# The last output product of a hybrid SSD/attention layer: who multiplies by the final norm weight, where the first two row tiles are finished, and which queue stores them

## The chip, the core and the metric

The kernel runs on one core of one Trainium2 chip. The time is device microseconds of one execution; the kernel before was run three times, and the median of these is what a change is measured against. Profiles come from one further execution each. The kernel uses five engines side by side, each with its own list of instructions in the order in which they were compiled: PE (TensorE, matrix products; the profile lists its weight loads as PEld), DVE (VectorE, elementwise), ACT (ScalarE, functions and scaled copies), POOL (GpSimd, elementwise) and SP (SyncE, which here only starts transfers). In this kernel ACT, POOL and SP start transfers (DMA). On-chip tiles have 128 partitions; PE's results go to eight banks of 128x512 float32.

## The reference

One layer with two branches (a state-space branch and an attention branch), both in float32, merged with gates, then one output product, a residual and a final RMSNorm. What matters here is only the end:

```python
merged = jax.nn.sigmoid(g_ssm) * (y @ w_proj_ssm) + jax.nn.sigmoid(g_attn) * (o @ w_proj_attn)
x = x + merged @ w_out                                  # (512, 2048) @ (2048, 2048)
y = x * lax.rsqrt(jnp.mean(x * x, axis=-1, keepdims=True) + EPS)
out = y * final_norm_w                                  # (512, 2048)
```

Each row of the output thus needs the sum of squares over all its 2048 columns before any part of it can be finished: the row factor r is one number for each row, the final weight one number for each column.

## The kernel before

**Tiles.** The 512 rows are four row tiles t = 0..3 of 128 rows, the 2048 columns four blocks b = 0..3 of 512. `res[t, b]` is one such 128x512 tile of x + merged @ w_out, kept on chip until the end. `ssf[:, t, b]` holds its sums of squares.

**Precision.** Each float32 operand is split into a rounded part h (a cast on ACT, line 433, written `wh`) and the rest l (a subtraction on DVE, line 434, written `wl`); a product is three matmuls (h·h, h·l, l·h). A weight chunk is 128x1024; PE can't use it before ACT has made `wh` and DVE has made `wl`. Each of these has three buffers.

**The output product.** Blocks 0 and 1 are made plainly (lines 1608-1624). Blocks 2 and 3 are made by Strassen's method with seven products instead of eight, in the order P1, P5, P6, P2, P3, P7, P4 (`Strassen.pair(1)`, lines 664-732), each of 48 matmuls on two banks with four weight chunks. P2 completes tiles (0,2) and (1,2), P3 completes (0,3) and (1,3), P7 completes (2,3) and (3,3), P4 completes (2,2) and (3,2). Each completed tile goes through `done_o` (lines 1642-1646): add x (line 1644), sum of squares on ACT (line 1576), `weigh`. The tiles of x for t < 2 are fetched by POOL into a three-buffer ring shared with the scratch of the squares (`fetch_o`, line 1632; the profile writes `gate<-x`); for t >= 2 they come with the final weight into one tile `fw` (`final_weights`, lines 1648-1655), which ACT's queue loads after P2.

P3 and P7 share the chunks Y: P3 uses each one, then POOL starts a transfer that adds a further block of w_out into it in place (line 505, `Y<-wo`), and P7 splits the sum again. P4 is made row tile by row tile (`product_rows`): its weights are split well ahead into `keep`, the first bank (t = 2) is complete half-way, the second (t = 3) at the end.

**The finish.** `weigh(t, b)` multiplies res[t, b] by the final weight on POOL (line 1571), in place, for all tiles but (2,2) and (3,2); the tiles of blocks 0 and 1 wait in the list `unweighed` until the weight is there and are all issued after P2. `finish(t)` sums the four sums of squares, makes r with a square root on ACT and a few one-column operations on DVE (lines 1659-1663, 185-191), scales the four tiles by r (two on DVE, two on ACT) and starts four stores of 256 KB, two from SP and two from ACT (line 1672). Row tiles 0 and 1 are finished in `before` of `last_o`, ahead of P4's sums and in an order that may not be changed (`pinned`); row tiles 2 and 3 as their banks of P4 complete (`each`).

**Order.** PE's order is written out by hand. All other engines' orders are made by a planner ahead of time: it walks through the program with a cost model, and whenever an engine is free in that model it takes, of the instructions that the model has ready, the one earliest in the program. `tc.high_priority(offset=n)` lets an instruction count as standing n instructions earlier (60 for the splits, `AHEAD`); `tc.keep_in_program_order` pins one. On the chip each engine then keeps this order, whatever really becomes ready first.

Of the kernel before, what the change touches and what calls it, by code (L numbers as in the profile page):

```python
# [15 lines left out]
ALU = mybir.AluOpType  # L16
AX = mybir.AxisListType

P = 128
D = 2048  # L20
SEQ = 512
# [51 lines left out]
def build(tc, a):  # L73
    nc = tc.nc
    act, dve, pool, pe = nc.scalar, nc.vector, nc.gpsimd, nc.tensor
# [25 lines left out]
    def few(n):  # L101

        n_small[0] += n
        assert n_small[0] <= 96
        return small[:, n_small[0] - n:n_small[0]]
# [36 lines left out]
    def mm(n="mm"):  # L142
        return ps.tile([P, SEQ], F32, tag="mm", bufs=3, name=n)

    def pa(n="pa"):
        return ps.tile([P, SEQ], F32, tag="pa", bufs=2, name=n)

    def pb(n="pb"):
        return ps.tile([P, SEQ], F32, tag="pb", bufs=2, name=n)

    def pc(n="pc"):
        return ps.tile([P, SEQ], F32, tag="pc", bufs=1, name=n)
# [50 lines left out]
    for t in range(TT):  # L203
# [7 lines left out]
        v = few(1)  # L211
# [169 lines left out]
    def st(name):  # L381
        return gp.tile([P, SEQ], F32, tag="st", bufs=3, name=name)
# [147 lines left out]
    def sum_tile(tag):  # L530

        if tag == "kk" or tag == "u" and kk:
            return kk.tile([P, SEQ], F32, tag="kk", bufs=2, name=tag)
        return part_.tile([P, SEQ], F32, tag=tag, bufs=2, name=tag)
# [14 lines left out]
    def product_done():  # L549
        for e in later:  # L550
            e[0] -= 1
        while later and later[0][0] <= 0:
            later.popleft()[1]()
# [31 lines left out]
    def product_rows(name, op, chunk, keep, each, pre):  # L585

        used.append((used[-1] + 1) % 4)
        bs = [b(name) for b in SETS[used[-1]]]
        for m in range(4):
            with tc.high_priority(offset=AHEAD):  # L590
                split_into(keep[0][:, m], keep[1][:, m], chunk(m))
        pre()
        for i in range(2):
            for j in range(8):
                xh, xl = op(0, j, i), op(1, j, i)
                wh, wl = (t[:, j // 2, j % 2 * 512:(j % 2 + 1) * 512] for t in keep)
                pe.matmul(bs[i], xh, wh, start=(j == 0), stop=False)
                pe.matmul(bs[i], xh, wl, start=False, stop=False)
                pe.matmul(bs[i], xl, wh, start=False, stop=(j == 7))
                yield 3  # L600
            each(i, bs[i])
# [275 lines left out]
    def rsqrt1(v):  # L877

        return small_rsqrt(v, 1, lambda n: hi.tile([P, 1], F32, tag={"rt": "mx", "rr": "nm"}[n], bufs=4, name=n))
# [490 lines left out]
    def place(shape, name):  # L1370

        n = n_places[0] % 5
        n_places[0] += 1
        return xb.tile(shape, F32R, tag="opb" if n else "opc", bufs=4 if n else 1, name=name)
# [58 lines left out]
    m_ops, m_op = Ops(m_d), {}  # L1433
# [112 lines left out]


    ssf = few(16).rearrange("p (t b) -> p t b", t=TT)
    res, room, unweighed = {}, {}, []

    def x_of(t, b):
        return a["x"][t * P:(t + 1) * P, b * SEQ:(b + 1) * SEQ]

    def out_chunk(acc, t, kc, h, l, start, stop):

        for k in range(2):
            kk_ = kc * 2 + k
            op = m_ops.view[f"x{t // 2 + 1}{kk_ // 8 + 1}"]
            mh, ml = (op(s_, kk_ % 8, t % 2) for s_ in range(2))
            wh, wl = (w_[:, k * SEQ:(k + 1) * SEQ] for w_ in (h, l))  # L1560
            pe.matmul(acc, mh, wh, start=(start and k == 0), stop=False)
            pe.matmul(acc, mh, wl, start=False, stop=False)
            pe.matmul(acc, ml, wh, start=False, stop=(stop and k == 1))

    def w_out(cg, kc):
        return w_split(w_load(w_tile("w"), "wo", 0, kc // 4, cg, kc % 4))

    def weigh(t, b):
        if t < 2 or b != 2:
            if "fw" in room:  # L1570
                pool.tensor_mul(res[t, b], res[t, b], room["fw"][:, b])
            else:
                unweighed.append((t, b))

    def squares(t, b):
        act.activation(st("scr"), res[t, b], AF.Square, accum_out=ssf[:, t, b:b + 1])

    def m_sums(q):
        ks = slice(4 * q, 4 * q + 4)

        def stored(w, tag):
            t = col_tile(tag, w)
            nc.sync.dma_start(t, m_d[w][:, q * 1024:(q + 1) * 1024])
            return t

        def whole(w, tag):
            t = col_tile(tag, w)
            dve.tensor_add(view4(t), m_op[w][:, 0, ks].bitcast(F32), m_op[w][:, 1, ks].bitcast(F32))
            return t

        def keep(w, t):
            split_into(m_op[w][:, 0, ks], m_op[w][:, 1, ks], view4(t))

        x21, x11 = stored("x21", "X"), stored("x11", "X")
        x22 = whole("x22", "Y")
        dve.tensor_sub(x22, x21, x22)
        keep("S1", x22)
        dve.tensor_sub(x21, x11, x21)
        keep("S3", x21)
        dve.tensor_sub(x11, x22, x11)  # L1600
        keep("S2", x11)
        x12 = whole("x12", "Y")
        dve.tensor_add(x12, x12, x11)
        return x12
# [3 lines left out]
    for cg in range(2):  # L1608
        accs = [pa("f"), pa("f"), pb("f"), pb("f")] if cg == 1 else [mm("f"), mm("f"), mm("f"), pc("f")]
        for t in range(TT):  # L1610
            o = res[t, cg] = sum_tile((("p1", "p5"), ("ms", "kk"))[cg][t // 2])
            act.dma_start(o, x_of(t, cg))
        for n, kc in enumerate(ORDER):
            h, l = w_out(cg, kc)
            for t in range(TT):
                out_chunk(accs[t], t, kc, h, l, n == 0, n == 7)
            if cg == 0 and n == 1:
                product_done()
            if (cg, n) in ((0, 5), (1, 2)):
                s4.append(m_sums(cg))  # L1620
        for t in range(TT):
            dve.tensor_add(res[t, cg], res[t, cg], accs[t])
            squares(t, cg)
            weigh(t, cg)
    m_ops.raws["S4"] = s4
    m_place("S4")()
    m_split("S4")()
# [11 lines left out]
    def x_late(t, b):  # L1639
        return fetched[t, b] if t < 2 else room["fw"][:, 2 * (b - 2) + 2 + t]  # L1640

    def done_o(t, b, o):
        res[t, b] = o
        dve.tensor_add(o, o, x_late(t, b))
        squares(t, b)
        weigh(t, b)

    def final_weights():
        t_ = room["fw"] = xa.tile([P, 8, SEQ], F32, tag="opa", bufs=2, name="fw")
        act.dma_start(t_[:, 0:4], a["fnw"].rearrange("o (b n) -> o b n", b=4).broadcast_to([P, 4, SEQ]))  # L1650
        for t in (2, 3):
            for b in (2, 3):
                act.dma_start(x_late(t, b), x_of(t, b))
        for t, b in unweighed:
            weigh(t, b)

    def finish(t, pinned=False):
        v = few(1)
        i = dve.tensor_reduce(v, ssf[:, t, :], AX.X, ALU.add)
        if pinned:  # L1660
            tc.keep_in_program_order(i)
        dve.tensor_scalar(v, v, 1.0 / D, EPS, ALU.mult, ALU.add)
        r = rsqrt1(v)
        for b in (2, 0, 1, 3):
            o = res[t, b]
            if b == 2 and t >= 2:
                dve.scalar_tensor_tensor(o, o, r, room["fw"][:, b], ALU.mult, ALU.mult)
            elif b == 1 or b == 2:
                dve.tensor_scalar_mul(o, o, r)
            else:  # L1670
                act.activation(o, o, AF.Copy, scale=r)
            (nc.sync if b % 2 == 0 else act).dma_start(a["out"][t * P:(t + 1) * P, b * SEQ:(b + 1) * SEQ], o)

    def last_o(name, op, chunk, u):
        keep = [place([P, 4, 1024], f"keep{i}") for i in range(2)]

        def before():
            for i in range(2):
                dve.tensor_add(u[i], x_late(2 + i, 2), u[i])
            for t in range(2):  # L1680
                finish(t, True)

        def each(i, bank):
            res[2 + i, 2] = u[i]
            dve.tensor_add(u[i], u[i], bank)
            squares(2 + i, 2)
            finish(2 + i)

        yield from product_rows(name, op, chunk, keep, each, before)

    wo = Strassen("wo", m_ops, 1, done_o, fetch_o, {(1, "P2"): [final_weights]}, kept_o, last_o)
    used.extend([0, 0, 3])
    run(wo.pair(1))
    manual.__exit__(None, None, None)
# [68 lines left out]
```

## Time and profile before

| | |
|---|---|
| median of 3 runs | 2035.28 us (2035.03 to 2037.79) |
| the profiled execution's own time | 2030.31 us |
| its span, first to last instruction | 2028.5 us |
| PE busy | 1947.4 us, 96% |
| DVE / ACT / POOL busy | 1526.9 / 987.6 / 335.7 us |
| granted TensorE clock, mean | 0.99 |
| the seven products of blocks 2 and 3, and the finish | from about 1929 us to the end |

How to read it: a row of the timeline gives the start in us from the span's start, the duration in us, the engine, the line of the kernel, the operation, out<-in, the shape, how many instructions were merged (their common length stands as the duration), and in brackets how long the engine was idle before it and what it then waited for. A tile is written by its program name without a buffer number; `big` is the tile of blocks 2 and 3, `p`, `ms` and `kk` are the tiles of blocks 0 and 1, `scr` is the squares' scratch. Engines with a q (POOLq, ACTq, SPq) are the queues' own rows, where DMA issues of ACT and SP stand.

### The profile page before, as it was taken

What the parts mean: (1) busy time and instruction counts of PE and PEld (TensorE: products, weight loads), DVE (VectorE), ACT (ScalarE), POOL (GpSimd) and SP (SyncE); (2) the same over time, 40 slices, a digit from 0 to 9 for tenths busy, and PEclk for the clock granted to TensorE, in tenths of its full rate; (3) what the DMA queues carried; (4) which work ended last, traced back from release to release, by engine and by line L of the source; (5) the groups of instructions that cost most, each with busy time, mean ns of one, the idle gap of its engine ahead of it and who ended that gap; (6) DMA issues with size and microseconds to landing.
All of it is one profiled execution on the core that took longest, in us unless ns stands there. A gap on an engine that the chain in (4) does not pass through costs nothing.

```text
span 2028.5 us, 24741 instructions
## 1 busy us (share of the span) xinstructions
PE 1947.4 (96%) x9026; PEld 1610.0 (79%) x9026; DVE 1526.9 (75%) x2000; ACT 987.6 (49%) x1374; POOL 335.7 (17%) x367
## 2 busy tenths in 40 slices
PE   6999999999999999999999999999999999999995
PEld 5888888888878778777788878888877788888884
DVE  7976676676759879899687577676676899789385
ACT  6444445444444655545546444444455455454353
POOL 0001001001032242243331111110021110100013
PEclk9999999999999999999999999999999999999998
DMA  5468558558456747686574857782389787848434
GB/s 192 166 185 207 161 130 207 158 133 208 125 172 173 234 145 205 215 243 202 162 203 146 242 168 200 200 229 87 91 217 312 230 284 275 275 149 272 120 86 142
DMA packets 168651, 382.78 MB, mean 189 GB/s; under 512 B 16272, under 2 KB 65552, under 8 KB 168336
## 3 DMA queue, kind: packets, MB, share of 16 engines
q1 hardware_dynamic: 102384, 232.03, 35.2%
q0 software_dynamic: 29824, 102.25, 22.9%
q10 hardware_dynamic: 36320, 46.91, 6.5%
q8 instruction: 71, 1.16, 0.2%
q14 instruction: 52, 0.43, 0.1%
HBM read 329.22 MB, written 98.04 MB: 211 GB/s over the span
## 4 chain that ended last, share of the span: by engine, by line
PE 61%; DVE 16%; issue 10%; DMA 8%; ACT 3%; POOL 1%; SPq 0%; ACTq 0%; DVEq 0%; POOLq 0%
PE P L579 9%; PE P L580 9%; PE P L578 9%; DVE wl L434 2%; PE za L168 2%; PE za L169 2%; PE za L170 2%; DVE sum L1052 2%; PE xbc L168 2%; PE xbc L169 2%; PE xbc L170 2%; DMA wraw<-wps 2%; DVE wl L164 2%; PE pb L1329 1%; PE qkv L170 1%
## 5 line engine op out<-in xcount | busy, mean ns | idle before, releaser
L433 ACT CAST wh<-X 128x1024 fp32r<-128x1024 f32 x164 | 172.4, 1054 | 196.0 <-PE P L580 149.8
L434 DVE TENSOR_TENSOR wl<-X,wh 128x1024 fp32r<-128x1024 f32 x164 | 199.9, 1223 | 89.5 <-ACT wh L433 89.2
L164 DVE TENSOR_TENSOR wl<-wraw,wh 128x1024 fp32r<-128x1024 f32 (+2 forms) x148 | 176.5, 1193 | 86.4 <-ACT wh L163 81.8
L163 ACT CAST wh<-wraw 128x1024 fp32r<-128x1024 f32 (+2 forms) x150 | 145.0, 969 | 134.6 <-PE za L169 36.7
L434 DVE TENSOR_TENSOR wl<-Y,wh 128x1024 fp32r<-128x1024 f32 x88 | 108.5, 1235 | 68.8 <-ACT wh L433 68.8
L433 ACT CAST wh<-Y 128x1024 fp32r<-128x1024 f32 x88 | 92.6, 1054 | 124.8 <-PE P L580 102.8
L168 PE MATMUL xbc<-h_h,wh 128*128 128x512 f32 x384 | 152.5, 397 | 0.0
L170 PE MATMUL xbc<-h_h,wl 128*128 128x512 f32 x384 | 150.7, 392 | 0.0
L169 PE MATMUL xbc<-h_l,wh 128*128 128x512 f32 x384 | 150.7, 392 | 0.0
L578 PE MATMUL P<-wh,h_h 128*128 128x512 f32 x384 | 149.4, 389 | 0.0
L579 PE MATMUL P<-wl,h_h 128*128 128x512 f32 x384 | 149.4, 389 | 0.0
L580 PE MATMUL P<-wh,h_l 128*128 128x512 f32 x384 | 149.4, 389 | 0.0
L434 DVE TENSOR_TENSOR wl<-wraw,wh 128x1024 fp32r<-128x1024 f32 x68 | 83.2, 1223 | 63.5 <-ACT wh L433 63.5
L433 ACT CAST wh<-wraw 128x1024 fp32r<-128x1024 f32 x68 | 71.6, 1053 | 116.1 <-PE P L580 61.8
L579 PE MATMUL P<-wl,S 128*128 128x512 f32 x288 | 112.3, 390 | 0.2 <-DVE wl L434 0.2
L580 PE MATMUL P<-wh,S 128*128 128x512 f32 x288 | 112.1, 389 | 0.0
L578 PE MATMUL P<-wh,S 128*128 128x512 f32 x288 | 112.1, 389 | 0.0
L168 PE MATMUL za<-h_h,wh 128*128 128x512 f32 x256 | 102.1, 399 | 0.0
L170 PE MATMUL za<-h_h,wl 128*128 128x512 f32 x256 | 100.5, 393 | 0.0
L169 PE MATMUL za<-h_l,wh 128*128 128x512 f32 x256 | 100.4, 392 | 0.0
L1052 DVE TENSOR_TENSOR_SCAN sum<-da,scn 128x512 f32<-128x512 f32 x64 | 89.0, 1403 | 0.0
L170 PEld LDWEIGHTS xbc<-h_h,wl 128*128 128x128 f32 x384 | 72.8, 190 | 15.7
(738 smaller groups left out, 5215.0 us busy)
## 6 DMA issues: line engine op xcount, KB each, us to landing
wraw<-wi SPq DMA_DIRECT2D x102, 512.0 KB, 4.1
T_wps<-wps POOLq DMA_DIRECT2D x32, 512.0 KB, 6.4
da<-da_d SPq DMA_DIRECT2D x64, 256.0 KB, 4.5
T_wpa<-wpa POOLq DMA_DIRECT2D x32, 512.0 KB, 9.6
wraw<-wps SPq DMA_DIRECT2D x24, 512.0 KB, 5.7
wraw<-wo SPq DMA_DIRECT2D x20, 512.0 KB, 3.7
xbc_d<-xbc ACTq DMA_DIRECT2D x24, 256.0 KB, 3.0
wraw<-wun SPq DMA_DIRECT2D x16, 384.0 KB, 3.2
```

Source lines behind the costliest of these rows:

```text
L163: act.copy(h, raw)
L164: (dve if ahead[0] else pool).tensor_sub(l, raw, h.bitcast(F32))
L168: pe.matmul(out, wh, xh, start=start, stop=False)
L169: pe.matmul(out, wh, xl, start=False, stop=False)
L170: pe.matmul(out, wl, xh, start=False, stop=stop)
L433: i = act.copy(hi_, raw)
L434: dve.tensor_sub(lo_, raw, hi_.bitcast(F32))
L578: pe.matmul(bs[i], xh, wh, start=(j == 0), stop=False)
L579: pe.matmul(bs[i], xh, wl, start=False, stop=False)
L580: pe.matmul(bs[i], xl, wh, start=False, stop=(j == 7))
L1052: dve.tensor_tensor_scan(sums[dd], flat(da), mask, 0.0, ALU.add, ALU.mult)
L1329: pe.transpose(tp[:, k * P:(k + 1) * P], prs[t][:, k * P:(k + 1) * P], ident)
```

## The change

Four things.

1. POOL multiplies by the final weight no more. Tiles of row tiles 0 and 1 get weight and row factor in one DVE instruction in `finish` (`scalar_tensor_tensor`: (o * r) * weight). Tiles (2,0), (2,1), (3,0), (3,1), (2,3), (3,3) get the weight by a DVE multiplication (`weigh`) as before by POOL's, and r in `finish` as before. Tiles (2,2) and (3,2) stay as they were.
2. `finish(0)` is called after P3 (in P3's hook, with the four multiplications of blocks 0 and 1 ahead of it), and `finish(1)` after P7, both unpinned, instead of ahead of P4's sums.
3. The stores of row tiles 0, 1 and 2 are all started by SP; those of row tile 3 by SP and ACT as before.
4. In P4 the addition and the squares of the second bank count as standing 12 instructions earlier.

```diff
     def weigh(t, b):
-        if t < 2 or b != 2:
-            if "fw" in room:
-                pool.tensor_mul(res[t, b], res[t, b], room["fw"][:, b])
-            else:
-                unweighed.append((t, b))
+        if t >= 2 and b != 2:
+            dve.tensor_mul(res[t, b], res[t, b], room["fw"][:, b])
...
             squares(t, cg)
-            weigh(t, cg)
...
-        for t, b in unweighed:
-            weigh(t, b)
-
-    def finish(t, pinned=False):
+
+    def finish(t):
         v = few(1)
-        i = dve.tensor_reduce(v, ssf[:, t, :], AX.X, ALU.add)
-        if pinned:
-            tc.keep_in_program_order(i)
+        dve.tensor_reduce(v, ssf[:, t, :], AX.X, ALU.add)
         dve.tensor_scalar(v, v, 1.0 / D, EPS, ALU.mult, ALU.add)
         r = rsqrt1(v)
         for b in (2, 0, 1, 3):
             o = res[t, b]
-            if b == 2 and t >= 2:
+            if b == 2 or t < 2:
                 dve.scalar_tensor_tensor(o, o, r, room["fw"][:, b], ALU.mult, ALU.mult)
             elif b == 1 or b == 2:
                 dve.tensor_scalar_mul(o, o, r)
             else:
                 act.activation(o, o, AF.Copy, scale=r)
-            (nc.sync if b % 2 == 0 else act).dma_start(a["out"][t * P:(t + 1) * P, b * SEQ:(b + 1) * SEQ], o)
+            (nc.sync if t < 3 or b % 2 == 0 else act).dma_start(a["out"][t * P:(t + 1) * P, b * SEQ:(b + 1) * SEQ], o)
...
                 dve.tensor_add(u[i], x_late(2 + i, 2), u[i])
-            for t in range(2):
-                finish(t, True)
 
         def each(i, bank):
             res[2 + i, 2] = u[i]
-            dve.tensor_add(u[i], u[i], bank)
-            squares(2 + i, 2)
+            with tc.high_priority(offset=12 * i):
+                dve.tensor_add(u[i], u[i], bank)
+                squares(2 + i, 2)
             finish(2 + i)
...
-    wo = Strassen("wo", m_ops, 1, done_o, fetch_o, {(1, "P2"): [final_weights]}, kept_o, last_o)
+    wo = Strassen("wo", m_ops, 1, done_o, fetch_o, {
+        (1, "P2"): [final_weights],
+        (1, "P3"): [lambda: [weigh(t, b) for t in (2, 3) for b in (0, 1)], lambda: finish(0)],
+        (1, "P7"): [lambda: finish(1)]}, kept_o, last_o)
```

More of the change, by code (lines that the diff above doesn't have):

```diff
@@ L1548, in build @@
     ssf = few(16).rearrange("p (t b) -> p t b", t=TT)
-    res, room, unweighed = {}, {}, []
+    res, room = {}, {}
     def x_of(t, b):
```

## The prediction

> **What bounds the kernel now.** I read first the page's busy shares, then PE's timeline over the seven products, since an engine that is 96% busy can be helped only where it stands still.
>
> ```profile
> PE 1947.4 (96%) x9026; PEld 1610.0 (79%) x9026; DVE 1526.9 (75%) x2000; ACT 987.6 (49%) x1374; POOL 335.7 (17%) x367
> ...
> 1982.29 0.39 PE L578 MATMUL P<-wh,S__15483 128*128 128x512 f32 x1
> 1992.94 0.79 PE L579 MATMUL P<-wl,S__15483 128*128 128x512 f32 x1 [10.27 <-DVE wl L434]
> ...
> 1996.52 0.55 PE L578 MATMUL P<-wh,S__15483 128*128 128x512 f32 x1
> 1996.91 0.39 PE L579 MATMUL P<-wl,S__15483 128*128 128x512 f32 x1
> ...
> 2005.52 0.39 PE L597 MATMUL P<-keep,x__15388 128*128 128x512 f32 x1
> ...
> 2016.17 0.39 PE L599 MATMUL P<-keep,x__15388 128*128 128x512 f32 x1
> ```
>
> P3 ends and P7 begins at 1982.29, and after one matmul PE waits 10.27 us for DVE's first `wl`. Then nine matmuls (1992.94 to 1996.91) take 3.97 us instead of the 9 x 0.227 = 2.04 of the later spacing (47 steps from 2005.52 to 2016.17): a further 1.9 us. The last matmul ends at 2016.56, and 11.94 us of the 2028.5 us span come after it. So there are two pieces to win: the hole (12.2 us with the slow restart) and the tail (11.9 us). Next, what DVE and POOL did in the hole:
>
> ```profile
> 1976.53 1.22 DVE L434 TENSOR_TENSOR wl<-Y,wh 128x1024 fp32r<-128x1024 f32 x1
> 1981.13 0.69 DVE L630 TENSOR_TENSOR big<-big,P 128x512 f32<-128x512 f32 x1 [3.38 <-PE P L580]
> 1984.64 7.11 DVE L1644 TENSOR_TENSOR big<-big,gate 128x512 f32<-128x512 f32 x1 [2.83 <-DMA gate<-x]
> 1991.67 4.56 DVE L434 TENSOR_TENSOR wl<-Y,wh 128x1024 fp32r<-128x1024 f32 x3
> 1996.87 0.69 DVE L1644 TENSOR_TENSOR big<-big,gate 128x512 f32<-128x512 f32 x1
> ...
> 2007.36 1.63 DVE L1644 TENSOR_TENSOR big<-big,fw 128x512 f32<-128x512 f32 x1
> ```
>
> ```profile
> 1975.78 0.57 POOL L1632 DMA_DIRECT2D gate<-x x1 [0.34 <-DVE big L1644]
> 1978.04 0.85 POOL L505 DMA_DIRECT2D Y<-wo x1 [1.70 <-DVE wl L434]
> 1978.61 5.30 POOL L1571 TENSOR_TENSOR p<-p,fw 128x512 f32<-128x512 f32 x4
> ...
> 1988.48 2.71 POOL L1571 TENSOR_TENSOR big<-big,fw 128x512 f32<-128x512 f32 x2
> 1990.90 0.81 POOL L1632 DMA_DIRECT2D gate<-x x1
> ...
> 2007.14 1.30 POOL L1571 TENSOR_TENSOR big<-big,fw 128x512 f32<-128x512 f32 x1 [6.13 <-ACT scr L1576]
> ```
>
> DVE's order is L630, L1644 for tile (0,3), then P7's `wl`. L1644 waits for the x tile until 1984.64, and then takes 7.11 us where the same form takes 0.69 at 1996.87. It ends at 1991.75; POOL's block of ten multiplications ends at 1991.19, 0.56 us before. The row at 2007.36 repeats it in small: POOL ends at 2008.44, L1644 at 2008.99, again 0.55 us later. I read this as DVE held up while POOL multiplies. The second x tile stands behind the block too and is issued only at 1990.90.
>
> **Part 1, no multiplication on POOL.** The order ahead of the hole has no reason to move, so the x tile still lands at 1984.64. L1644 then takes 0.69 and ends at 1985.33; before, the first `wl` began at 1991.67 and PE 1.27 us later, so PE starts at 1985.33 + 1.27 = 1986.60 instead of 1992.94: 6.3 us gained. The next `wl`, 1.22 each (row at 1976.53), come faster than PE eats a chunk (12 x 0.23 = 2.76). The second x tile is issued some 12 us earlier and is no longer late. Bounds of the landing, from the other transfers of that stretch (the issue's own length in ns, then us to landing; the last row is the window 1975 to 1982: busy time of PE, PEld, DVE, ACT and POOL, granted clock, DMA share, GB/s):
>
> ```profile
> L1632 POOL DMA_DIRECT2D gate<-x x2: 570/688/807, 1975.8 to 1990.9; - x2
> DMA to landing us min/median/max: 3.6/6.2/8.8
> L1653 ACTq DMA_DIRECT2D fw<-x x4: 335/666/812, 1975.5 to 1977.3; - x4
> DMA to landing us min/median/max: 8.2/10.9/11.6
> 1975.00:1982.00 7.00, 7.00 (x32) 5.79 (x31) 3.43 (x4) 3.72 (x7) 4.96 (x6) 1.00 1.01 223
> ```
>
> The DMA engines are full from 1975 to 1982 (share 1.01), and no transfer of it goes away. At 3.6 us the tile would be there at 1979.4, before L630 ends, and PE would wait until 1981.82 + 0.69 + 1.27 = 1983.8 (2.8 us more gained); at 11.6 us it lands at 1987.4 (2.8 us lost). I take 8.8, its own row.
>
> The slow restart: a hole of 10.65 - 6.34 = 4.3 us start to start is left, 3.9 us idle. The other holes of the trace:
>
> ```profile
> 952.81 1.97 PE L1073 MATMUL yb<-xT,G 128*128 128x64 f32 x8 [2.94 <-DVE G L1063]
> 954.54 0.77 PE L168 MATMUL qkv<-h_h,wh 128*128 128x512 f32 x1
> ...
> 958.95 0.51 PE L169 MATMUL qkv<-h_l,wh 128*128 128x512 f32 x1
> ...
> 1182.52 0.39 PE L1244 MATMUL vp<-wh,ckv_h 128*128 128x256 f32 x1 [2.75 <-ACT za L405]
> ```
>
> After 2.94 us idle the following matmuls run at 0.43 spacing until 958.95; after 2.75 us they don't. 3.9 lies above both, so I keep the 1.9 us; the other end is a gain of 1.9. The Trainium skill, TensorE: Matmul & The Clock Gate, section "HAM oscillation", asks for no PE gap over about 3.4 us; by it too the restart stays slow, while the row at 1182.52 alone would make it 1.9 us better (about 2024.7 at the end).
>
> DVE has to carry the new work without keeping P7's `wl` waiting. The prices:
>
> ```profile
> L1667 DVE SCALAR_TENSOR_TENSOR big<-big,rr,fw 128x512 f32<-128x512 f32 x2 | 1.5, 748 | 0.0
> L1669 DVE TENSOR_SCALAR ms<-ms,rr 128x512 f32<-128x512 f32 x2 | 1.0, 482 | 0.0
> 2009.76 1.28 ACT L185 ACT_TABLE_LOAD   x1
> 2020.72 0.16 DVE L1659 TENSOR_REDUCE small<-small 128x1 f32<-128x4 f32 x1 [2.26 <-ACT scr L1576]
> ```
>
> Added: six multiplications at 0.69 (4.1 us), eight scalings at 0.75 (6.0) for four at 0.48 (1.9): DVE +8.2 us, while ACT loses four scalings (about 0.7 each). From 1984.64 to P7's end (2005.52 - 6.3 = 1999.2) there are 14.5 us; in them go L1644 twice and L630 (2.1), four `wl` (4.9), four multiplications (2.8) and `finish(0)` (L1659 to the first scaling, 1.6, and four scalings, 3.0): 14.4. It just fits, and the 3.4 us that DVE idles before 1981.13 are a reserve for the multiplications. P7's splits count as 60 instructions earlier, so they go first where they are ready. Cost taken: 0. The cover gone, it is the last `wl` that slips: P7's fourth chunk is wanted 8.3 us after its start, so a DVE queue that is 2 to 5 us behind costs PE as much. ACT's table load (1.28) comes with `finish(0)` into P7, beside casts that ACT does with room. Nothing to cost: SP's queue, on which six stores more stand before no load of this stretch, at some 0.4 us an issue.
>
> **Parts 2 to 4, the tail.** Before, all sixteen stores (4.2 MB) and all four finishes came after 2010. Row tiles 0 and 1 now go out during P7 and P4. What is left behind the last matmul:
>
> ```profile
> 2017.78 0.68 DVE L1685 TENSOR_TENSOR big<-big,P 128x512 f32<-128x512 f32 x1
> ...
> 2019.37 0.70 ACT L1671 ACTIVATE big<-big,rr 128x512 f32<-128x512 f32 x1
> 2019.98 0.61 ACT L1576 ACTIVATE scr<-big 128x512 f32<-128x512 f32 x1
> 2020.50 0.19 ACT L1576 ACTIVATION_READ_ACCUMULATOR scr<-big 128x1 f32 x1
> ...
> 2022.31 0.72 ACT L1671 ACTIVATE p<-p,rr 128x512 f32<-128x512 f32 x1 [1.00 <-DVE rr L191]
> 2022.94 0.71 ACT L1671 ACTIVATE big<-big,rr 128x512 f32<-128x512 f32 x1
> 2023.94 0.41 ACTq L1672 DMA_DIRECT2D out_dram<-big  x1
> ```
>
> The chain bare of waits: addition 0.69, squares 0.80, factor 1.59 (2020.72 to 2022.31), scalings to the last issue 1.63 (to 2023.94), store to the end 4.56: 9.3 us, with some 0.2 between engines 9.5, against 11.94. The difference of 2.4 us is the addition, 1.2 us late behind older scalings, and ACT's squares, which began 1.5 us after it behind row tile 2's scalings. Bounds: the sixteen stores landed in 2.3 to 4.8 us (row below), so up to 2 us less in an emptier system. On the other side DVE: in P4 (10.9 us) stand P7's six results (4.1), two multiplications (1.4), L1679's two additions (1.4), `finish(1)` (4.6), the first bank's addition (0.7) and `finish(2)` (2.8): 15.0, so up to 4 us could stand in front of the last addition. The 12 instructions that it is brought forward should put it before most. I take 2.4.
>
> ```profile
> DMA to landing us min/median/max: 2.3/3.5/4.8
> ```
>
> **Sum.** 6.3 + 0 + 2.4 = 8.7 us. The profiled execution took 2030.31 (span 2028.5 and 1.8 around it), so its like would take 2021.6. The median of the runs stands 5.0 us above that execution; I carry the difference over: 2035.28 - 8.7 = 2026.6. The forecast's own range, with the clock, landing and tail ends (-1.9, ±2.8, -2/+4): 2022 to 2031.
>
> **Rivals.**
>
> *The stall goes altogether* (0.17). If the new DVE work shifts the planner's picture so that P7's first `wl` comes ahead of L1644, PE waits only until about 1983.5; the hole and the slow restart go, 10.65 + 1.9 - 1.2 = 11.3, with the tail 13.7: 2021.6. For it: the splits stand 60 instructions ahead. Against: the planner had them behind L1644 until now.
>
> *DVE becomes the bound* (0.17). The 14.4 of 14.5 us don't fit, `finish(0)` waits on ACT for the root and its table, the fourth `wl` is 3 us late, and the 4 us of backlog in P4 eat the tail's 2.4 and 1.6 more: 8.7 - 3 - 4 = 1.7 gained, 2033.6; half of that slippage gives 2030.
>
> *POOL was not the holder* (0.08): the change takes its multiplications away and L1644 still sits there until something else lands. For it: the trace names only the DMA; against: the 0.56 and 0.55 us. Then only the tail moves: 2032.9. The Trainium skill, SBUF — State Buffer, section "SBUF: two separate sides", has VectorE and GpSimd lock a shared port for one instruction each; by that alone L1644 would have waited for one POOL operation (1.3 us at 2007.14), and some 5 of the 6.3 us would have another cause. The trace's 7.11 us, to the end of the block, speak against so short a wait.
>
> *Slower* (0.08): the queue order on DVE puts the four multiplications and `finish(0)` between L1644 and P7's first `wl`. PE then waits for 2.8 + squares 0.8 + root and factor 1.6 + table 1.28 + 3.0 = 9.5 us more: 3.2 later than before; and with the same order in P4 the last addition 4 us late against 2.4 gained: +1.6. Together +4.8: 2040.1. It decides once more than 8.7 us stand ahead of the first `wl` and the last addition. For it: these instructions are unpinned, and DVE keeps the planned order even where a transfer lands later than planned, as L1644's 2.83 us show. Against: the 60 instructions.
>
> **How the numbers follow.** Forecast 0.50, and the rivals as given. 0.2% (4 us) is about what a measurement of this kernel can tell from no change: faster means under 2031.2. Forecast, first rival and half of the second: 0.75; the other half and the third: 0.17; the fourth: 0.08. The range takes in the first rival's 2021.6 with its unknown tail and the second and third up to 2034: 2020 to 2034.
>
> **What would show it.** L1644 for (0,3) at 0.69 us with no POOL row beside it; PE's hole before P7's second matmul near 4 us; P7's other `wl` without a PE wait; the first row tiles' stores from about 1995; the last matmul near 2010 and some 9.5 us behind it. Wrong would be a hole as before, new PE waits for `wl` in P7, or L1685's second row more than 2 us behind the last matmul.

## The result, and the profile after

The changed kernel takes 2024.99 us (median of 18 runs, 2018.77 to 2031.17); the kernel before, run beside it, takes 2032.70 us (18 runs, 2027.22 to 2037.79). The ratio is 0.9964, with a 95% interval of 0.9952 to 0.9975: 7.3 us faster, between 5.1 and 9.8. The profiled execution took 2028.84 us, with a span of 2027.1. First the page's busy shares, then PE, DVE and ACT's queue over the same stretch as before (start, duration, engine, line, operation; idle time and releaser in brackets):

```profile
PE 1951.1 (96%) x9026; PEld 1610.9 (79%) x9026; DVE 1523.9 (75%) x2010; ACT 985.2 (49%) x1370; POOL 318.6 (16%) x353
```

```profile
1988.14 0.39 PE L578 MATMUL P<-wh,S__15483 128*128 128x512 f32 x1
1993.49 0.80 PE L579 MATMUL P<-wl,S__15483 128*128 128x512 f32 x1 [4.96 <-DVE wl L434]
...
1996.22 0.58 PE L579 MATMUL P<-wl,S__15483 128*128 128x512 f32 x1
...
1996.87 0.40 PE L578 MATMUL P<-wh,S__15483 128*128 128x512 f32 x1
...
2016.39 0.39 PE L599 MATMUL P<-keep,x__15388 128*128 128x512 f32 x1
...
1987.20 0.68 DVE L630 TENSOR_TENSOR big<-big,P 128x512 f32<-128x512 f32 x1
1991.61 0.69 DVE L1640 TENSOR_TENSOR big<-big,gate 128x512 f32<-128x512 f32 x1 [3.73 <-DMA gate<-x]
1992.22 3.49 DVE L434 TENSOR_TENSOR wl<-Y,wh 128x1024 fp32r<-128x1024 f32 x3
...
2001.95 0.75 DVE L1659 SCALAR_TENSOR_TENSOR big<-big,rr,fw 128x512 f32<-128x512 f32 x1
...
2013.26 0.68 DVE L1676 TENSOR_TENSOR big<-big,P 128x512 f32<-128x512 f32 x1
...
2016.37 0.75 DVE L1659 SCALAR_TENSOR_TENSOR big<-big,rr,fw 128x512 f32<-128x512 f32 x1
2017.04 0.48 DVE L1661 TENSOR_SCALAR kk<-kk,rr 128x512 f32<-128x512 f32 x1
2017.44 0.68 DVE L1676 TENSOR_TENSOR big<-big,P 128x512 f32<-128x512 f32 x1
...
2022.20 0.47 ACTq L1664 DMA_DIRECT2D out_dram<-big  x1
```

The addition of x to tile (0,3), now line 1640, takes 0.69 us instead of 7.11, and PE's hole shrinks from 10.27 to 4.96 us. What is left is a wait for the x tile, behind which P7's splits stand on DVE. From P7's first matmul to P4's last there are 28.25 us where there were 33.88: 5.6 won. The last matmul ends at 2016.78, and 10.3 us follow it where 11.9 did: 1.6 won. Together 7.25 us, as much as the runs show. (The two spans differ by only 1.4 us because P7 began 5.85 us later in this execution, at 1988.14 instead of 1982.29.)

The chain of waits (start, length, what) tells what bounds the end now:

```profile
1981.62 9.89 DMA gate<-x
...
1998.71 0.72 ACT scr L1573 x2
1999.45 1.28 ACT L185
...
2002.01 0.69 DVE big L1659
2002.70 0.66 DVE p L1659
...
2012.14 0.66 DVE big L1671 x2
...
2013.26 0.69 DVE big L1676
```

Up to 1997.5 it runs through PE; then it goes over to ACT, and from 2002.01 through DVE's scalings, additions and weights one after the other, up to the first bank's addition. ACT's part is this:

```profile
1997.76 1.05 ACT L433 CAST wh<-Y 128x1024 fp32r<-128x1024 f32 x1 [4.64 <-PE P L580]
1998.71 0.63 ACT L1573 ACTIVATE scr<-big 128x512 f32<-128x512 f32 x1
...
1999.45 1.28 ACT L185 ACT_TABLE_LOAD   x1
2000.74 0.30 ACT L185 ACTIVATE rt<-small 128x1 f32<-128x1 f32 x2
```

Row tile 0's mean square is ready on DVE at 1997.09, but its root stands on ACT's list behind P7's fourth cast, which waits for PE, and behind the squares of tile (1,3). So it comes at 2000.74, together with row tile 1's (the x2), and the scalings bunch up on DVE late in P7. From there to the first bank's addition DVE's queue sets the end, though not by much: the second bank's addition begins 0.66 us after the last matmul. The windows of P4's first 7.5 us show DVE busy throughout (length, then busy time and instructions of PE, PEld, DVE, ACT, POOL, granted clock, DMA share, GB/s), the changed kernel first, the one before second:

```profile
2005.70:2013.20 7.50, 7.50 (x34) 6.20 (x34) 7.50 (x13) 1.45 (x4) 0.00 (x0) 1.00 0.42 154
```

```profile
2005.52:2013.00 7.48, 7.48 (x34) 6.19 (x33) 6.49 (x16) 3.87 (x9) 2.81 (x2) 1.00 0.00 1
```

### The profile page after: what moved, and what is told of

Read it like the earlier page. It is cut to its first block, busy times and chain, and to the rows that moved or that the text cites. A ratio compares the mean times of both kernels' runs of the same rounds, so it can differ in the third digit from the quotient of the medians.

```text
span 2027.1 us, 24730 instructions
## 1 busy us (share of the span) xinstructions
PE 1951.1 (96%) x9026; PEld 1610.9 (79%) x9026; DVE 1523.9 (75%) x2010; ACT 985.2 (49%) x1370; POOL 318.6 (16%) x353
## 4 chain that ended last, share of the span: by engine, by line
PE 60%; DVE 17%; issue 10%; DMA 8%; ACT 3%; POOL 1%; SPq 0%; DVEq 0%; POOLq 0%; ACTq 0%
PE P L579 9%; PE P L580 9%; PE P L578 9%; PE za L168 2%; PE za L169 2%; PE za L170 2%; DVE sum L1052 2%; DVE wl L434 2%; PE xbc L168 2%; PE xbc L169 2%; PE xbc L170 2%; DVE wl L164 2%; DMA wraw<-wps 1%; PE pb L1329 1%; PE qkv L170 1%
```

## The experiments

Single executions differ by several us before P7 has begun: its first matmul starts between 1974.2 and 1990.9 us in these profiles. So beside each ratio stands the stage itself, read from PE's timeline: the largest wait at P7's start, the time from P7's first matmul start to P4's last, what is left after the last matmul, and the sum of the last two (with 0.4 for the last matmul), all in us.

| kernel | hole | P7 to P4's end | after it | sum | ratio to before, interval |
|---|---|---|---|---|---|
| before | 10.27 | 33.9 | 11.9 | 46.2 | 1 |
| changed | 4.96 | 28.3 | 10.3 | 39.0 | 0.9964 [0.9952, 0.9975] |
| e1, part 1 alone | 3.77 | 28.5 | 14.3 | 43.1 | 0.9975 [0.9959, 0.9991] |
| e2, parts 2 to 4 alone | 10.26 | 34.4 | 9.4 | 44.1 | 0.9981 [0.9964, 0.9997] |
| e3, before, POOL's multiplications doubled | 9.32 and 6.86, before P7's last chunk | 41.3 | 13.1 | 54.7 | one run |
| e9, before with early x | 10.08 | 33.7 | 11.8 | 45.9 | 0.9993 [0.9982, 1.0003] |
| e8, changed with early x | 1.06 | 22.9 | 10.9 | 34.2 | 0.9934 [0.9915, 0.9953] |
| e5, changed, x by SP | 3.25 | 27.8 | 9.7 | 38.0 | 0.9935 [0.9914, 0.9957] |
| e14, changed, two scalings on ACT | 0.47 | 22.3 | 11.9 | 34.6 | 0.9924 [0.9907, 0.9942] |
| e15, e14 with early x | 0.47 | 22.3 | 10.4 | 33.1 | 0.9926 [0.9907, 0.9945] |
| e6, changed, old stores | 4.57 | 28.9 | 10.3 | 39.6 | one run |
| e10, changed, 10 idle on POOL | 5.15 | 33.6 | 11.6 | 45.6 | one run |
| e11, the same, chained | 5.97 | 30.2 | 10.6 | 41.2 | one run |
| e12, e10 without four DVE weights | 10.26 | 33.5 | 10.0 | 43.9 | one run |

The ratios of e1, e2 and the changed kernel can't be told apart by their intervals; what each does is read from its stage. Those of e5 and e14 gain more (13 and 15 us) than their stages do (8.2 and 11.6); where the rest comes from is not shown.

**The two halves, each alone (e1, e2).**

- e1: `weigh` on DVE for t >= 2, one scaling with r and weight for t < 2; `finish`, its place and its queues as before.
- e2: `finish(0)` after P3, `finish(1)` after P7, SP's stores, the 12 instructions; `weigh` on POOL as before.

> The kernel before with part 1 of the change alone: the final weight put on by DVE, all four finishes and their stores where they were. Theory (POOL's block of multiplications held DVE): PE's hole between P7's first and second matmul shrinks from 10.3 us idle to about 5.0, as in the changed kernel, the addition of the x tile takes 0.69 us; the tail behind the last matmul stays at 12 us or grows by 1 to 2, since eight scalings are dearer on DVE; time 4 to 6 us below before. Rival (POOL was not the holder, a transfer was): the hole stays near 10, time as before.

> The kernel before with parts 2 to 4 alone: row tile 0 finished after P3 and row tile 1 after P7, stores of row tiles 0 to 2 by SP, the weight still put on by POOL. Theory: the hole stays at 10 to 11 us idle with the addition of about 7 us in it, the tail falls from 11.9 to about 10.3; time 1 to 3 us below before. Rival (the early finish is what shortens the hole, or the two parts need each other): the hole shrinks below 7, or the tail stays at 12.

Part 1 shortens the hole, and only part 1: it is 3.77 us in e1 and 10.26 in e2, and the products take 28.5 and 34.4 us. But alone it makes the tail 2.3 us longer, since the dearer scalings of row tiles 0 and 1 are then still near the end. In e1 row tile 1's four scalings begin only after the last matmul, which ends at 2010.13, and row tile 3's factor (the sum at 2015.45) stands behind them:

```profile
2011.74 0.75 DVE L1665 SCALAR_TENSOR_TENSOR big<-big,rr,fw 128x512 f32<-128x512 f32 x1
...
2015.45 0.15 DVE L1657 TENSOR_REDUCE small<-small 128x1 f32<-128x4 f32 x1
```

Parts 2 to 4 alone win 2.6 us in the tail. By the sums, e1 wins 3.1 and e2 2.1, both together 7.25: the second half also removes what the first half costs. Of parts 2 to 4 it is the early finishes that win: the stores' queue moves the tail by 0.01 us (e6 below), and the 12 instructions leave the compiled program of the changed kernel as it is.

**Is POOL the holder? (e9, e3)** e9 is the kernel before, with the x tiles of block 3 loaded early by SP into free weight buffers, so that line 1648 (1644 before) waits for no transfer. e3 doubles POOL's multiplications, so that the weight is applied twice in the tiles where POOL applies it.

```diff
-        if t < 2:
+        if t < 2 and b == 3:
+            with tc.high_priority(offset=LOAD_AHEAD):
+                fetched[t, b] = wp.tile([P, 1024], F32, tag="wraw", bufs=3, name="xearly")[:, :SEQ]
+                nc.sync.dma_start(fetched[t, b], x_of(t, b))
+        elif t < 2:
```

> The kernel before with nothing changed but the fetch of the two x tiles of block 3: SP loads them some 20 us earlier into free weight buffers, so that no transfer is late; POOL's multiplications stay. Theory (POOL holds DVE): the addition starts at once after P3's first result, about 3 us earlier, is held to the end of POOL's block all the same, about 10 us long, and PE's hole stays at 10 us; time within 1 us of before. Rival (the late transfer makes the hole): the addition takes 0.69 us, the hole falls to about 2, time 8 to 10 us below before.

> The kernel before with each of POOL's multiplications by the final weight made twice (so these tiles are weighted twice). Theory (DVE gets in only when POOL's whole block is done): the block of ten becomes twenty, some 12.6 us longer, and the addition of the first x tile ends with it again, about 20 us long instead of 7.1; PE's hole about 23 us idle. Rival (DVE waits for one POOL operation only): the addition stays at 7 us or less and the hole at about 10.

The timeline of e9:

```profile
1987.24 0.69 DVE L630 TENSOR_TENSOR big<-big,P 128x512 f32<-128x512 f32 x1 [3.38 <-PE P L580]
1987.96 9.71 DVE L1648 TENSOR_TENSOR big<-big,xearly 128x512 f32<-128x512 f32 x1
...
1987.02 2.81 POOL L1571 TENSOR_TENSOR p<-p,fw 128x512 f32<-128x512 f32 x2
...
1994.38 2.73 POOL L1571 TENSOR_TENSOR big<-big,fw 128x512 f32<-128x512 f32 x2
...
1998.86 0.80 PE L579 MATMUL P<-wl,S__15483 128*128 128x512 f32 x1 [10.08 <-DVE wl L434]
```

The x tile is there, the addition starts 0.7 us after L630 (3.5 before), and lasts 9.71 us, until 0.56 us after POOL's block (1997.67 against 1997.11). The hole and the time don't move. So it is not the x tile's transfer that holds it. e3 was a partial miss: the planner put P7's first splits ahead, and there DVE and POOL took turns, while a later split was held:

```profile
1986.48 6.17 DVE L434 TENSOR_TENSOR wl<-Y,wh 128x1024 fp32r<-128x1024 f32 x3 [1.91 <-ACT wh L433]
...
2008.49 7.62 DVE L434 TENSOR_TENSOR wl<-Y,wh 128x1024 fp32r<-128x1024 f32 x1 [10.12 <-ACT wh L433]
...
2007.42 1.04 ACT L433 CAST wh<-Y 128x1024 fp32r<-128x1024 f32 x1 [14.86 <-DMA Y<-wo]
```

Its 2047.34 us (one run) hold two prices: the split of 7.62 us, and a transfer into Y that POOL issues only behind its multiplications.

**When does POOL hold DVE, and when do they take turns? (e10, e11, e12)** All three are the changed kernel with ten more multiplications on POOL whose results nobody uses, where POOL's block stood before: e10 independent, e11 each on the last one's result. e12 is e10 without `weigh` for blocks 0 and 1 of row tiles 2 and 3.

```diff
+        idle = [wp.tile([P, 1024], F32, tag="wraw", bufs=3, name=f"idle{i}") for i in range(2)]
+        spots = [u[:, h * SEQ:(h + 1) * SEQ] for u in idle for h in range(2)]
+        for n in range(10):
+            pool.tensor_mul(spots[n % 4], t_[:, 0], t_[:, 1])   # e11: spots[0] <- spots[0], t_[:, 1]
```

> The changed kernel with ten idle POOL multiplications of 128x512 added after the final weight's load, into free buffers, each independent of the one before. Theory (DVE gets at two on-chip inputs only in a break of POOL's stream): the first DVE operation with two such inputs that comes while they run, one of the four weight multiplications, is held to about 0.6 us after the end of the ten, some 12 us long; PE's hole 10 us or more. Rival (DVE waits for one operation): none over 2.5 us, hole about 5 to 8.

> The same ten POOL multiplications, each reading what the one before wrote, so that each has to wait for it. Theory (a break of the stream lets DVE in): the two engines take turns; DVE's operations beside them take 1.5 to 2.5 us each, none is held longer, and POOL's too stretch to 2 us; PE's hole 5 to 8 us. Rival (the whole block holds whatever it is made of): one DVE operation of 10 us or more, as with the independent ten.

> The changed kernel with the ten idle POOL multiplications (the same independent ones as before), but without the weight multiplications of tiles (2,0), (2,1), (3,0), (3,1), so that the final weight is missing in these four tiles of the output. DVE then stands idle where POOL's ten begin. Theory (who comes first decides: a stream that begins while DVE has no operation of two on-chip inputs under way keeps DVE out until it ends): POOL's ten operations are 1.5 to 1.6 us long at 1.22 spacing, the addition of x to tile (0,3) lasts until some 0.5 us after the tenth (5 to 10 us), and PE's hole in P7 is 8 to 11 us. Rival (the form of the multiplications decides, and independent ones take turns): as in the run with all of DVE's multiplications, the addition lasts 0.7 to 1.8 us, the splits 2.3 us each, POOL's operations 1.3 to 2.3 us, the hole 4 to 6 us.

The timeline of e10, then of e12:

```profile
1983.61 0.68 DVE L1570 TENSOR_TENSOR kk<-kk,fw 128x512 f32<-128x512 f32 x1
...
1988.76 0.94 DVE L1640 TENSOR_TENSOR big<-big,gate 128x512 f32<-128x512 f32 x1 [2.82 <-DMA gate<-x]
1989.62 6.71 DVE L434 TENSOR_TENSOR wl<-Y,wh 128x1024 fp32r<-128x1024 f32 x3
...
1982.74 17.25 POOL L1653 TENSOR_TENSOR idle<-fw 128x512 f32<-128x512 f32 x10
1999.92 0.59 POOL L1628 DMA_DIRECT2D gate<-x  x1
```

```profile
1985.23 0.69 DVE L630 TENSOR_TENSOR big<-big,P 128x512 f32<-128x512 f32 x1 [3.38 <-PE P L580]
1988.97 6.87 DVE L1640 TENSOR_TENSOR big<-big,gate 128x512 f32<-128x512 f32 x1 [3.06 <-DMA gate<-x]
...
1982.71 12.58 POOL L1653 TENSOR_TENSOR idle<-fw 128x512 f32<-128x512 f32 x10
...
1997.04 0.80 PE L579 MATMUL P<-wl,S__15483 128*128 128x512 f32 x1 [10.26 <-DVE wl L434]
```

e10 went against the theory that a stream of independent operations without a break is enough: DVE's addition took 0.94 us, the splits 2.3 each, and POOL's ten stretched to 17.25 us. e11 took turns too: the addition took 1.78 us, the splits 2.2 each, POOL's 2.1 beside them. (e10's sum is large mostly for another reason: the second x tile is issued behind POOL's ten, at 1999.92, and P7 has a second hole of 3.12 us.) In e12 POOL's list is the same, only DVE's four weight multiplications are gone, so that DVE is idle where POOL begins: POOL's ten need 12.58 us, DVE's addition is held for 6.87, until 0.55 us after the tenth, and the hole is 10.26 us, that of before. So POOL's stream on data that nobody else uses is enough to make the hole, and between these two runs it is how the stream begins that decides whether it holds DVE or takes turns.

**What is left of the hole (e8, e5).** e8 is the changed kernel with e9's early x tiles; e5 fetches them at the same point, by SP instead of POOL.

```diff
-            pool.dma_start(fetched[t, b], x_of(t, b))
+            (nc.sync if b == 3 else pool).dma_start(fetched[t, b], x_of(t, b))   # e5
```

> The changed kernel with the two x tiles of block 3 loaded by SP some 20 us earlier into free weight buffers. Theory (what is left of the hole after the change is the late x tile alone): the addition starts as soon as P3's first result and the four weight multiplications are done, PE's hole falls from 5.0 to 1 to 2 us idle and the 1.6 us of slow restart go; first to last matmul of P7 and P4 in about 23 us instead of 28.2; time some 5 us below the changed kernel, about 0.994 of before. Rival (the chunks Y, whose transfers share the full DMA engines, are next in line): hole 3 to 4 us, gain under 2 us.

> The changed kernel with the same two x tiles fetched at the same moment as before, into the same buffers, but by SP's queue instead of POOL's. Theory (the tile is late because it stands behind the three transfers into Y on POOL's queue): it lands in 4 to 6 us instead of 9.9, the hole falls to 0 to 2 us idle, time 4 to 5 us below the changed kernel. Rival (it is late because all DMA engines are full, whatever the queue): landing 8 to 10 us, hole 4 to 5 us, time as the changed kernel.

The timeline of e8:

```profile
1986.74 0.69 DVE L1644 TENSOR_TENSOR big<-big,xearly 128x512 f32<-128x512 f32 x1
...
1988.62 0.50 PE L579 MATMUL P<-wl,S__15483 128*128 128x512 f32 x1 [1.06 <-DVE wl L434]
```

With the tile there, the hole is 1.06 us, the slow restart is gone, and 5.3 us more are won in the products. The same early load was worth nothing before the change (e9). With another queue alone (e5) neither the theory nor the rival came true whole. The first tile landed after 8.5 us, just below the 8.7 to 9.9 of POOL's queue in the changed kernel, e1, e6 and e14 (the second one after 11.8), so one execution shows no clear effect of the queue. The hole fell to 3.25 us, but the stretch is only 0.4 us shorter, since the slow restart behind it cost 2.8 us instead of 1.6. An issue some 20 us earlier (e8), while the DMA engines were at a share of 0.32 (1965 to 1972), landed in 2.8 to 3.1 us.

**Order and DVE's load (e14, e15), and the stores (e6).** In e14 tiles (1,0) and (1,1) get the weight with the four others after P3, and r from ACT. The planner then puts three of P7's splits ahead of the addition of x; the tile still takes 9.1 us to land. e15 adds e8's early tiles. e6 goes back to the old stores.

```diff
-        if t >= 2 and b != 2:
+        if t >= 2 and b != 2 or t == 1 and b < 2:
...
-            if b == 2 or t < 2:
+            if b == 2 or t == 0 or t == 1 and b == 3:
...
-            elif b == 1 or b == 2:
+            elif b == 1 and t != 1:
...
-        (1, "P3"): [lambda: [weigh(t, b) for t in (2, 3) for b in (0, 1)], lambda: finish(0)],
+        (1, "P3"): [lambda: [weigh(t, b) for t in (1, 2, 3) for b in (0, 1)], lambda: finish(0)],
```

> The changed kernel, but tiles (1,0) and (1,1) get the weight by a DVE multiplication together with the four of row tiles 2 and 3, and their row factor from ACT: two scalings of 0.75 us fewer on DVE in P4. The planned order on DVE changes with it: three of P7's splits now stand ahead of the addition of x to tile (0,3); they stood behind it. Theory (what is left of the hole is DVE standing in line behind a late x tile): the hole before P7's second matmul goes from 5.0 to 1.5 us or less, no slow restart, P7's first to P4's last matmul start 22.9 to 23.5 us instead of 28.25, about 2019.5 us as a run. Rival (the split itself is late, for its chunk or for ACT's cast): the hole stays at 3 to 5 us and the 28.25 within 1.5. The tail: if DVE's backlog in P4 made the second bank's addition 0.66 us late, it now begins within 0.3 us of the last matmul's end and 9.6 to 9.9 us are left; if the stores set the tail, it stays at 10.3.

> As the last, and SP loads the two x tiles of block 3 early. If the order alone takes the hole away, the early x tile adds nothing: P7's first to P4's last matmul start within 0.5 us of the last kernel's, the run's ratio within 0.1% of it. If the late x tile still costs something in another place (finish(0) late, DVE's queue in P7), this one is 1 to 3 us shorter in that stretch. Tail 9.6 to 10.0, where the early x tile alone had 10.93 with the second addition 1.4 us late.

> The changed kernel with the stores of row tiles 0, 1 and 2 started by SP and ACT in turn, as before the change. If the queue of the stores matters in the tail (ACT's issues of 0.4 us stand between its squares and scalings, or SP's four last stores stand behind row tile 2's), the tail after the last matmul moves by more than 0.4 us from 10.32; if not, it stays between 10.0 and 10.7 and the last matmul where the hole puts it (P7's first to P4's last start 27.5 to 29).

The timeline of e14, and the window of its P4 up to the first bank's addition:

```profile
1985.47 2.35 DVE L434 TENSOR_TENSOR wl<-Y,wh 128x1024 fp32r<-128x1024 f32 x2
...
1989.80 0.68 DVE L1640 TENSOR_TENSOR big<-big,gate 128x512 f32<-128x512 f32 x1
...
1986.74 0.50 PE L579 MATMUL P<-wl,S__15483 128*128 128x512 f32 x1 [0.47 <-DVE wl L434]
...
2008.19 0.39 PE L599 MATMUL P<-keep,x__15388 128*128 128x512 f32 x1
...
2006.65 0.69 DVE L1676 TENSOR_TENSOR big<-big,P 128x512 f32<-128x512 f32 x1
...
2010.43 0.48 DVE L1661 TENSOR_SCALAR kk<-kk,rr 128x512 f32<-128x512 f32 x1
2010.83 0.68 DVE L1676 TENSOR_TENSOR big<-big,P 128x512 f32<-128x512 f32 x1
```

```profile
1997.50:2007.30 9.80, 9.80 (x45) 8.08 (x44) 9.80 (x16) 2.04 (x5) 0.00 (x0) 1.00 0.63 215
```

The order alone takes the hole away (0.47 us, 22.3 for the products), with the same late tile. The tail was a miss: 11.9 us instead of 9.6 to 9.9. PE ends 5.9 us sooner in its stage, but DVE is busy without a gap up to 2007.3, and the second bank's addition starts 2.25 us after the last matmul. So 1.6 of the 5.9 us are given back. In e15 the products take the same 22.3 us; but `finish(0)` can start scaling 9.5 us after P7's start instead of 10.8 (1988.37 and 1996.66), and the tail is 1.5 us shorter. The runs of e14 and e15 can't be told apart. With the old stores (e6) the tail stays at 10.3: the chain from the last addition to the last issue is 0.25 us longer there (5.01 against 4.76), but the addition begins 0.25 us sooner after the last matmul.

By the sums of their stages e8, e14 and e15 beat the changed kernel by 4.3 to 5.8 us. The intervals of e14 and e15 lie below its own, that of e8 touches it; the medians are 2019.78, 2018.9 and 2018.03 us.

## Why the prediction was right, and where it was off

**POOL holds L1644: right.** The addition takes 0.69 us as soon as POOL has no block beside it, and e1, e9 and e12 show that the block is the cause: without it the hold is gone, with the x tile there it stays, and with a block on idle data it comes back. The Trainium skill, SBUF — State Buffer, section "SBUF: two separate sides", has the engine that starts first keep the shared port for one whole instruction. e10's splits of 2.3 us beside POOL (1.22 alone) agree with that; the holds of 6.87 and 9.71 us over whole blocks don't.

**6.3 us for the hole: 5.6 measured.** The term that was off is the x tile's landing: taken as 8.8 us, it was 9.89 in this execution, so that the hole was 4.96 us idle instead of 3.9. It lay within the bounds of 3.6 to 11.6. The slow restart was kept at 1.9 us and measured 1.6: from 1993.49 to 1996.87 PE starts eight times in 3.38 us, which takes 1.8 at 0.227. That this fits so well is partly luck, since after holes of 3.25 us and more the same loss lies between 1.5 and 3.0 us in the other runs. The prediction's ground for keeping it, that 3.9 us lies above a length between 2.75 and 2.94, doesn't hold: such a length isn't there (last section).

**0 for DVE's new work in P7: right for PE, wrong for what follows.** PE meets no second wait in P7. But `finish(0)` was to fit in well before P7's end, in a sum that counted DVE's time alone. Its root had to wait for ACT's list (P7's fourth cast, tile (1,3)'s squares, the table load), so its scalings begin only at 2001.95 and run nearly to P7's end at 2005.7. From 2000.97 DVE has no gap until 2013.94.

**2.4 us for the tail: 1.6 measured.** The step that failed is that the 12 instructions would put the last addition ahead of most of DVE's queue. It starts at 2017.44, 0.66 us after the last matmul, behind two scalings of `finish(2)`, which are late because the first bank's addition waited its turn: the bank was complete at 2011.34, the addition began at 2013.26. The 12 instructions change nothing: the compiled program is the same with and without them. The chain from there to the last issue took 4.76 us, 0.15 less than forecast, and the last store 4.9 us to the end (2022.20 to 2027.1) instead of 4.56. The bound of 4 us for the DVE backlog was the right mechanism; e14 shows it at 2.25 us, once PE is no longer late.

**The rivals.** "POOL was not the holder" is refuted by e9. "The stall goes altogether" did not happen here, since the planner left the splits behind the addition; e14 makes exactly its condition true, and its products are 11.6 us shorter than before (33.9 to 22.3), where the rival put 11.3. "DVE becomes the bound" came true in part: not in P7, but from 2002 on, at a price of some 0.7 us. "Slower" did not happen: nothing of `finish(0)` stood ahead of P7's first split.

**What would show it.** The last matmul was to come near 2010 and the first stores from about 1995. They came at 2016.78 and 2002.72; less the 5.85 us by which P7 began later in this execution, that is 2010.9 and 1996.9.

**The time.** 7.7 us between the medians against 8.7 forecast. The forecast of 2026.6 also carried the three runs' median of 2035.28, 2.6 us above that of the 18 runs; the two errors go against each other and leave 1.6 us, and that part is luck. The range of 2022 to 2031 is narrower than its three ends added up, which give 2020 to 2033; 2024.99 lies in both.

## What to carry to other kernels

Where an operation lasts ten times its usual length, look for what another engine ran until its end: POOL was busy for only 17% of the time, and its multiplications cost the critical path more than the same work on DVE does. Of two causes in a row only the last one pays: the early x tile was worth nothing while POOL held DVE, and 5 us afterwards. And when a hole is closed, read which engine bounds the stretch behind it: in e14 a quarter of the gain went back to DVE's queue.

## What the runs showed of the hardware that was not expected

**A stream of POOL multiplications has two forms.** In the form that holds DVE, the single operations of 128x512 start every 1.22 us and are 1.5 to 1.6 us long, so that each overlaps the next by 0.3 (before, e2, e9's block, the second block of e3, e12). In the other they are 1.25 to 1.3 us long with hardly any overlap while alone, and with DVE at work the two alternate, 2.1 to 2.3 us for each (e10, e11, the first block of e3). Single operations on POOL, not merged (start and length), of e12 and of e10:

```
e12  1982.71 1.59   1983.97 1.58   1985.22 1.57   1986.48 1.53   1987.70 1.52
e10  1982.74 2.70   1985.42 1.28   1986.67 1.25   1987.89 1.26   1989.11 1.71   1990.79 2.25
```

The holding streams of before, e2, e9 and e12 are of independent operations, and all holding streams, e3's second block too, stood right behind a transfer issue on POOL, with DVE idle. e10's stood there too, but began during one of DVE's multiplications, and its first operation lasted 2.70 us; so for such a stream e10 and e12 show that DVE's state at the start decides. DVE idle is not enough. The first two multiplications of e9 and the first block of e3 began with DVE idle too, but after a wait for the weight's load instead of an issue, and had the other form. The last nine of e11 began with DVE idle and behind an issue, but each reads the one before, and they took turns. Why these three conditions matter, and that the overlap itself keeps DVE out, is not shown.

**The hold depends on DVE's inputs.** L630, which reads one input from PE's banks, takes 0.69 us in the middle of POOL's block (1987.24 in e9, 1985.23 in e12); the additions and splits with two on-chip inputs are the ones that are held.

**The slow restart of PE.** After every hole of P7 that lasted 3.25 us or more, the next matmuls start 0.43 us apart for a while; in the changed kernel the granted clock is 0.50 from 1993.49 to 1996.63 and 1.00 from 1996.87 on. After 1.06 us (e8) and 0.47 us (e14, e15) they don't. In between the length of the hole doesn't decide. The same hole of 2.75 us at line 1244 is followed by starts 0.12 us apart in the kernel before and, from the fifth on, by starts 0.21 to 0.22 apart in the changed one (granted clock 0.50 from 1180.88 on). The hole of 2.94 us at line 1073 is followed by slow starts in the kernel before and by normal ones in e2 (granted clock 1.00 from 950.08 to 953). After e10's second hole, 3.12 us, the first two steps are 0.34 and 0.23 us, as after a short hole, and the next eight 0.37 to 0.43. The loss doesn't grow with the hole either: 1.5 us after 10.26 (e12), 1.6 after 4.96 (changed), 3.0 after 3.77 (e1). What decides is not shown. The Trainium skill, TensorE: Matmul & The Clock Gate, section "HAM oscillation", gives about 3.4 us as the longest gap that is safe; slow starts after 2.75, 2.94 and 3.25 us go against that, and the measurement decides.
